# Three PSUM tiles for attention scores and two for the large products, weight sums started behind the first attention, operand forms split by quarters

## The chip, the cores and the metric

The kernel runs on one core of one Trainium2 chip. Its time is the device time of one execution in microseconds (us), the median of three runs. All times below are in us unless marked otherwise.

## The reference

One layer of a hybrid decoder is computed for a prompt of 2048 tokens and for 8 samples of 4 tokens, width 1024, in fp32. Cut to what matters:

```python
h = rms_norm(x, norm_pre_mix)
q, k, v, z1, z2, g_a, g_b = project_inputs(h, w_in, b_gate)   # w_in: 1024 x 5376
for gi, (win, dil) in enumerate(((128, 1), (512, 4), (2048, 16))):
    o, lse = dilated attention of 4 heads of 64 (prompt: banded, sample: against the cache and the new rows)
o_a = merge_dilations(outs, lses)                 # softmax over the three groups' lse
o_b = z1 * (tril(w_spatial) @ layer_norm(z2) + b_spatial)
merged = g_a * (o_a @ w_ao) + g_b * (o_b @ w_bo)  # gates are sigmoids
x = x + rms_norm(merged @ w_out, norm_post_mix)
x = x + rms_norm(square(relu(rms_norm(x, norm_pre_ffn) @ w_up)) @ w_down, norm_post_ffn)
```

The outputs are the new x of prompt and samples, the k and v rows to keep, and the normalised rows of the gMLP.

## The kernel before

The prompt is worked in two halves of 1024 tokens, called stages s = 0 and s = 1; the 32 sample tokens ride with stage 0 (so its chunks are 3 of 352 columns, stage 1's are 2 of 512). Every large product is made of three TensorE matmuls per 128 rows of the contraction: each fp32 operand is split into a high and a low part, and high x high, high x low and low x high are added in PSUM (`gemm`, `gemm_rows`). The order of work is: for each of six head pairs and groups `project` (its v, q and k columns) with the `attention` of the pair before interleaved; `gmlp`; `mix` in stage 0 or `mix_seven` in stage 1 (the gates); `out_rows`; after stage 1 the MLP (`ffn`) for both halves. `mix_seven` and the MLP use a scheme of seven products in place of eight, for which sums of weight quarters (`s1` to `s4`) and differences of activation quarters (`t1`, `v`, `t3`, `t4`) are needed.

**PSUM.** There are eight tiles of 512 fp32 columns: two of tag "t" (transposes), and of the pool `po` three "g" (large products), two "s" (attention scores, and the `w_ao` products of the gates), one "u" (attention values). `bank(kind)` at L204 hands them out in turn: the first matmul of a product waits until the engine that read the tile's last product (ACT or DVE) is done.

**Lanes.** Work that is to lie between the matmuls of the large products is written as Python generators on four lanes. `tick` steps lanes 0 to 2 between rows of a product: lane 0 has the attention, lane 1 the merge, lane 2 the sample attention, whose keys and values come by DMA from the caches (`sample_attention`, DVE lines L919, L920, L956, L967). Lane 3 has `weight_sums`: the sums of weight quarters, made by DMA alone, DRAM to DRAM. A step of it issues one DMA of 512 KB, by turns a copy on SP's queue and an adding DMA on POOL's queue. `pace` (L308) counts the columns of the large products and steps lane 3 each time that another `SUM_EVERY` = 4250 are through. The counter starts at -3 x 4250. What is left over is issued ahead of the MLP.

**The order on the engines** is set by a scheduler that works from the program as written; each engine then takes its instructions in the order in which the scheduler put them.

**Attention.** `scores` (L708, L709) writes the two heads of a unit of 128 queries to one "s" tile; DVE reads it (L710: mask and minimum), ACT makes the exponentials (L714), TensorE transposes them (L742), and `values` (L756) multiplies. `project` writes the keys of the next pair to the two key slots (ACT L575, DVE L576, sample columns L583), which the scores of the pair before must have read. Its own matmuls are those of L322.

**The gates of stage 1.** `mix_seven` first makes the products with `w_ao` and `w_bo` for all eight blocks m, while `forms` makes four difference forms: t3 stays in SBUF, and v, t4 and t1 go by DMA to DRAM (`gt`). Then come 49 products of 12 matmuls (L1235), seven for each of the blocks m = 1 to 7. Each is read by one or two DVE adds (L1242) or an ACT copy (L1240), and gates are made by sigmoids on ACT (L1245). The first 14 products are those of m = 1 and 2 by turns. While they run, `stage` (L1149) brings a form back from DRAM in four quarters of 128 x 512, and `place` splits quarters into high (ACT L349) and low part (DVE L350). `PLACED` says ahead of which product which quarters of which form are split. v is used from product 6 on, t4 from product 8 on, t1 from product 12 on.

Of the kernel before, what the change touches and what calls it, by code (L numbers as in the profile page):

```python
# [42 lines left out]

SUM_EVERY = 4250

# [28 lines left out]

PLACED = {1: (0, (0, 1, 2, 3)), 4: (1, (0, 1)), 5: (1, (2, 3)), 8: (2, (0, 1)), 9: (2, (2, 3))}
FORMS = ("b11", "b21", "b22") + DIFFS
# [36 lines left out]
def hybrid_step(ctx: ExitStack, tc: tile.TileContext, ins: dict, outs: list):  # L113
# [87 lines left out]
    def bank(kind):  # L201
        return po[0].tile([P, 512], F32, tag=kind, bufs={"g": 3, "s": 2, "u": 1}[kind], name="p" + kind)

# [101 lines left out]

    calls = [-3 * SUM_EVERY]

# [707 lines left out]
    def gmlp(s):  # L1015
# [6 lines left out]
        def token_major(m, st):  # L1022
            cs = slice(m * P, (m + 1) * P)
            yield
            for hf in range(2):
# [7 lines left out]
                yield  # L1033
            if s == 0:
                pt = ps.tile([P, 512], F32, tag="t", name="pt")
                nc.tensor.transpose(pt[:NSMP, :P], st[:, HALF:TMAX], ident)
                nc.scalar.activation(zs[:, cs], pt[:NSMP, :P], AF.Gelu)

        def layer_norm():
# [17 lines left out]
            if s == 0:  # L1057
                nc.sync.dma_start(sg_s[0].rearrange("b t c -> (b t) c"), zs)

        def gate(g):  # L1060
# [57 lines left out]
    def mix_seven():  # L1118
# [96 lines left out]
        for n, (m, i) in enumerate(seq):  # L1215
            if n in PLACED:
                place(*PLACED[n])
            if n in (2, 6):
                staged.append(stage(len(staged)))
# [24 lines left out]
            for q, o in done:  # L1244
                nc.scalar.activation(  # L1245
                    X[q], X[q], AF.Sigmoid, bias=b_gate[:, o + m : o + m + 1], scale=-1.0 if o else 1.0
                )
            if i in (4, 6):
                h = halves[i == 6]
                pb = sm.tile([P, 512], F32, tag="e0", name="pbx")  # L1250
                nc.sync.dma_start(pb, pb_d[m][:, h])
                nc.vector.tensor_tensor(out[:, h], out[:, h], a[:, h], ALU.mult)
                nc.vector.tensor_tensor(b[:, h], b[:, h], pb, ALU.mult)
                nc.gpsimd.tensor_tensor(out[:, h], out[:, h], b[:, h], ALU.add)
            if m == 7:

                for ks, h, upto in ((range(8), lo, 1), (range(4), hi, 2), (range(4, 8), hi, 5)):
                    for k in ks:
                        if (k < 7 and i == upto) or (k == 7 and i == (4 if h is lo else 6)):
                            split(act[:, k, 0, h], act[:, k, 1, h], row(order[k])[:, h], nc.vector)  # L1260
# [166 lines left out]
    def weight_sums():  # L1427
# [13 lines left out]
        todo = []  # L1441
        by_rows("w_up", up_d)
        w = ins["w_in"][0]
        ca, cb = (slice(o, o + D) for o in (3328, 4352))
        for q in range(4):
            u, l = slice(q * P, (q + 1) * P), slice(512 + q * P, 512 + (q + 1) * P)
            todo.append(parts(w[u, ca], w[l, ca], w[u, cb], w[l, cb], [gate_d[i, u] for i in range(4)]))
        by_rows("w_down", down_d)
        for n in range(len(todo) + 2):
# [499 lines left out]
```

## Time and profile before

| | |
|---|---|
| median of 3 runs (lowest, highest) | 2857.8 (2856.02, 2861.61) |
| the profiled execution | 2865.88, span 2864.2 |
| TensorE clock granted, mean | 0.995 |
| PE busy | 2810.6 (98%) |
| DVE, ACT, POOL busy | 1366.7 (48%), 1291.4 (45%), 1328.0 (46%) |
| DMA | 550.95 MB, mean 192 GB/s |

The stages lie in the span about so: start to 60, projections and attention of stage 0 to 345, `gmlp` to 430, `mix` to 716, `out_rows` to 836, projections and attention of stage 1 to 1180, `gmlp` to 1276, the first part of `mix_seven` to 1328, its seven-product part to 1470, `out_rows` to 1561, then the MLP. A row of the profile names the line, the engine, the operation and out<-in; an arrow <- behind a time names what ended the wait. PE is TensorE's matmuls, DVE is VectorE, ACT is ScalarE, POOL is GpSimd, and SP issues most DMAs. "x3" is a count.

### The profile page before, as it was taken

The numbers are of one execution on the slowest core, as the hardware profiler recorded it, in microseconds if no ns is written. First come the engines' busy times: TensorE is split into PE (matmuls) and PEld (weight loads), VectorE is DVE, ScalarE is ACT, GpSimd is POOL, SyncE is SP. The second block draws the span as 40 slices with busy tenths as digits, with TensorE's granted clock in tenths as the row PEclk, the third lists the DMA queues.
The fourth block names the chain that finished last, engine by engine and source line by source line (L and its number), as shares of the span: only waits on it lengthen the run. The fifth ranks groups of instructions, "written<-read, shape, count | busy, mean of one in ns | idle before, by whom it ended". The sixth has DMA issues, their size and how long they took to land.

```text
span 2864.2 us, 45829 instructions
## 1 busy us (share of the span) xinstructions
PE 2810.6 (98%) x17350; PEld 2557.5 (89%) x17350; DVE 1366.7 (48%) x2318; ACT 1291.4 (45%) x2519; POOL 1328.0 (46%) x1167
## 2 busy tenths in 40 slices
PE   8999999999999999999999999999999999999998
PEld 8999999999988888877888999999999888888887
DVE  4557555662463444454555546443434644452235
ACT  5344444213553444443446544553434545554333
POOL 3346535464314444344661444445556644445553
PEclk9999999999999999999999999999999999999999
DMA  5566645864667756558456869676656766686655
GB/s 190 162 186 166 174 128 141 227 180 122 203 183 203 209 131 155 126 130 241 136 156 235 283 222 311 191 253 204 203 193 215 223 206 193 190 277 197 191 187 170
DMA packets 486606, 550.95 MB, mean 192 GB/s; under 512 B 28273, under 2 KB 373425, under 8 KB 476658
## 3 DMA queue, kind: packets, MB, share of 16 engines
q1 hardware_dynamic: 472992, 502.60, 54.7%
q0 software_dynamic: 13248, 45.36, 8.8%
q8 instruction: 137, 2.24, 0.3%
q14 instruction: 83, 0.68, 0.1%
q10 hardware_dynamic: 146, 0.07, 0.0%
HBM read 425.54 MB, written 206.27 MB: 221 GB/s over the span
## 4 chain that ended last, share of the span: by engine, by line
PE 50%; DVE 2%; DMA 1%; issue 1%; ACT 1%; POOL 0%; SPq 0%; DVEq 0%; POOLq 0%; ACTq 0%
PE pd L1598 21%; PE pe L1598 11%; PE pe L1706 10%; PE pg L1235 4%; PE pg L336 2%; PE pg L322 1%; PE ps L322 0%; POOL wf L1509 0%; DVE act L350 0%; DMA gt<-gt 0%; PE pt L1310 0%; DMA raw<-in_w_up_dram 0%; ACT junk L395 0%; DMA flat<-hd 0%; DMA f<-ov 0%
## 5 line engine op out<-in xcount | busy, mean ns | idle before, releaser
L1509 POOL TENSOR_TENSOR wf<-raw,wf 128x512 fp32r<-128x512 f32 x493 | 696.6, 1416 | 733.3 <-ACT wf L1508 691.9
L322 PE MATMUL pg<-act,wh 128*128 128x352 f32 (+2 forms) x2976 | 798.6, 347 | 0.8 <-ACT act L349 0.8
L322 PEld LDWEIGHTS pg<-act,wh 128*128 128x128 f32 x2976 | 524.7, 190 | 31.0 <-POOL wl L303 1.1
L1508 ACT CAST wf<-raw 128x512 fp32r<-128x512 f32 x493 | 304.9, 619 | 535.7 <-PE pd L1598 185.7
L322 PE MATMUL pg<-act,wl 128*128 128x352 f32 (+3 forms) x1488 | 513.6, 346 | 0.0
L303 POOL TENSOR_TENSOR wl<-raw,wh 128x512 fp32r<-128x512 f32 (+1 forms) x184 | 242.4, 1345 | 312.9 <-ACT wh L299 270.0
L1598 PE MATMUL pd<-act,wf 128*128 128x264 f32 x2880 | 361.2, 285 | 1.4 <-ACT ov L196 1.0
L1598 PEld LDWEIGHTS pd<-act,wf 128*128 128x128 f32 x2880 | 354.0, 189 | 2.0 <-ACT ov L196 1.4
L322 PEld LDWEIGHTS pg<-act,wl 128*128 128x128 f32 x1488 | 281.5, 189 | 17.1
L1706 PE MATMUL pe<-wf,act 128*128 128x512 f32 (+1 forms) x984 | 224.3, 389 | 1.3 <-ACT wf L1508 1.0
L1706 PEld LDWEIGHTS pe<-wf,act 128*128 128x128 f32 x984 | 181.7, 188 | 43.0 <-ACT wf L1508 1.2
L1607 DVE TENSOR_TENSOR ov<-pd,ov 128x528 f32<-128x528 f32 x140 | 96.2, 704 | 193.5 <-PE pd L1598 188.0
L1598 PE MATMUL pd<-pair,wf 128*128 128x264 f32 x1440 | 183.2, 284 | 0.0
L1598 PE MATMUL pe<-act,wf 128*128 128x512 f32 x768 | 182.6, 392 | 0.1
L1509 DVE TENSOR_TENSOR act<-flat,act 128x1024 fp32r<-128x1024 f32 (+1 forms) x76 | 102.6, 1352 | 164.7 <-ACT act L1508 164.6
L1598 PEld LDWEIGHTS pd<-pair,wf 128*128 128x128 f32 x1440 | 177.9, 188 | 0.0
L1598 PEld LDWEIGHTS pe<-act,wf 128*128 128x128 f32 x768 | 143.8, 188 | 32.9 <-issue 0.3
L299 ACT CAST wh<-raw 128x1024 fp32r<-128x1024 f32 (+1 forms) x91 | 91.9, 1011 | 176.9 <-PE pg L322 101.9
L1607 DVE TENSOR_TENSOR ov<-pe,ov 128x512 f32<-128x512 f32 x136 | 91.5, 687 | 136.9 <-PE pe L1598 126.0
L714 ACT ACTIVATE ov<-ov 128x256 f32<-128x256 f32 (+1 forms) x192 | 91.8, 479 | 115.5 <-DVE ov L710 113.3
L710 DVE CUSTOM_DVE_ANT_0 ov<-ps,con 128x256 f32<-128x256 f32 (+1 forms) x192 | 72.4, 383 | 135.7 <-PE ps L709 124.2
L1598 PE MATMUL pd<-oa,wf 128*128 128x264 f32 x1056 | 135.0, 284 | 0.0
(340 smaller groups left out, 4673.2 us busy)
## 6 DMA issues: line engine op xcount, KB each, us to landing
raw<-in_w_in_dram SPq DMA_DIRECT2D x70, 512.0 KB
raw<-up_sums SPq DMA_DIRECT2D x128, 256.0 KB
raw<-down_sums SPq DMA_DIRECT2D x128, 256.0 KB
flat<-f SPq DMA_DIRECT2D x48, 528.0 KB
raw<-in_w_up_dram SPq DMA_DIRECT2D x96, 256.0 KB
raw<-in_w_down_dram SPq DMA_DIRECT2D x96, 256.0 KB
flat<-f SPq DMA_DIRECT2D x48, 512.0 KB
f<-ov SPq DMA_DIRECT2D x16, 1056.0 KB
```

The source lines that it names most:

```text
L299: nc.scalar.copy(wh[:, :o], raw[:, :o])
L303: eng.tensor_tensor(wl[:, c], raw[:, c], wh[:, c].bitcast(F32), ALU.subtract)
L322: nc.tensor.matmul(pt[:, :n], a[:, o : o + P], b, start=(i == 0 and j == 0), stop=(i == last and j == 2))
L336: nc.tensor.matmul(pt[:n, o : o + width], a, b, start=(i == 0 and j == 0), stop=(i == last and j == 2))
L710: nc.vector.tensor_tensor_reduce(pb[:, h, :w], sp[:, h, :w], mask[:, 2 * P - w : 2 * P], 1.0, 3.0e38, ALU.add, ALU.min, stats[:, u, h : h ...
L714: nc.scalar.activation(pb[:, h, :w], pb[:, h, :w], AF.Exp, scale=-1.0, bias=stats[:, u, h : h + 1], accum_out=stats[:, u, 2 + h : 3 + h],)
L1235: nc.tensor.matmul(pt, w[:, c, k], x[k][:, d], start=k == 0 and j == 0, stop=k == 3 and j == 2)
L1508: nc.scalar.copy(high, raw)
L1509: eng.tensor_tensor(low, raw, high.bitcast(F32), ALU.subtract)
L1598: nc.tensor.matmul(pt[:, o : o + n], w[:, a], x[:, b, c : c + n], start=first and j == 0, stop=last and j == 2)
L1607: nc.vector.tensor_tensor(X[to], res, X[add], ALU.add)
L1706: nc.tensor.matmul(pts[i][:, cs], x[k][:, c, t * P : (t + 1) * P], w[:, d, 0, cs], start=k == 0 and j == 0, stop=k == 15 and j == 2,)
```

## The change

Four things are changed together. (1) The pool `po` has two tiles "g" and three "s" in place of three and two. (2) `pace` starts at -200000 columns and steps every 3600, so that no sum is issued in the projections and the attention of stage 0; and the sums of the gate weights come first, then those of `w_up`, then `w_down`. (3) In `mix_seven` the first form is split one quarter ahead of each of products 1 to 4, the second two quarters ahead of products 6 and 7, the third ahead of 10 and 11; the second and third are fetched at products 4 and 8 instead of 2 and 6, and the first half of a block's rows is finished behind the sixth of its seven products instead of the fifth. (4) `token_major` has one more `yield` ahead of the transpose of the sample columns (stage 0), and `layer_norm` one at its end.

```diff
-SUM_EVERY = 4250
+SUM_EVERY = 3600
-PLACED = {1: (0, (0, 1, 2, 3)), 4: (1, (0, 1)), 5: (1, (2, 3)), 8: (2, (0, 1)), 9: (2, (2, 3))}
+PLACED = {
+    1: (0, (0,)), 2: (0, (1,)), 3: (0, (2,)), 4: (0, (3,)),
+    6: (1, (0, 1)), 7: (1, (2, 3)), 10: (2, (0, 1)), 11: (2, (2, 3)),
+}
     def bank(kind):
-        return po[0].tile([P, 512], F32, tag=kind, bufs={"g": 3, "s": 2, "u": 1}[kind], name="p" + kind)
+        return po[0].tile([P, 512], F32, tag=kind, bufs={"g": 2, "s": 3, "u": 1}[kind], name="p" + kind)
-    calls = [-3 * SUM_EVERY]
+    calls = [-200000]
             if s == 0:
+                yield
                 pt = ps.tile([P, 512], F32, tag="t", name="pt")
                 nc.tensor.transpose(pt[:NSMP, :P], st[:, HALF:TMAX], ident)
             if s == 0:
                 nc.sync.dma_start(sg_s[0].rearrange("b t c -> (b t) c"), zs)
+            yield
-            if n in (2, 6):
+            if n in (4, 8):
                 staged.append(stage(len(staged)))
-            if i in (4, 6):
+            if i in (5, 6):
                 h = halves[i == 6]
                 pb = sm.tile([P, 512], F32, tag="e0", name="pbx")
-                        if (k < 7 and i == upto) or (k == 7 and i == (4 if h is lo else 6)):
+                        if (k < 7 and i == upto) or (k == 7 and i == (5 if h is lo else 6)):
                             split(act[:, k, 0, h], act[:, k, 1, h], row(order[k])[:, h], nc.vector)
         todo = []
-        by_rows("w_up", up_d)
         w = ins["w_in"][0]
         ca, cb = (slice(o, o + D) for o in (3328, 4352))
         for q in range(4):
...
+        by_rows("w_up", up_d)
         by_rows("w_down", down_d)
```

The instructions of each engine are the same in number and kind, but for two loads of an activation table less on ACT; they stand in another order. Lines below `bank` have moved by 3 to 6, so L322 of before is L326 of after, and so on. Three places follow.

PE in stage 1, where one head pair's projection follows another (about 955 to 968 in the span before): ps are score tiles, pg large products, pu values, pt transposes; pair0 and pair1 are the two key slots. pg_9511 and pg_9560 are the two chunks of the next keys, pg_9599 is the first product behind them, and ps_9462 has the last scores that read the old keys. Before:

```order
L322 MATMUL pg_9560<-act_75,wl_9506 128x512
L322 MATMUL pg_9599<-act_75,wh_9593 128x512 x2
L322 MATMUL pg_9599<-act_75,wl_9594 128x512
L322 MATMUL pg_9599<-act_75,wh_9593 128x512 x2
L322 MATMUL pg_9599<-act_75,wl_9594 128x512
L322 MATMUL pg_9599<-act_75,wh_9593 128x512 x2
L322 MATMUL pg_9599<-act_75,wl_9594 128x512
L322 MATMUL pg_9599<-act_75,wh_9593 128x512 x2
L322 MATMUL pg_9599<-act_75,wl_9594 128x512
L756 MATMUL pu_9471<-ov_76 128x64 x2
L708 MATMUL ps_9462<-pair1_8411,oa_77 128x256
L709 MATMUL ps_9462<-pair1_8411,oa_77 128x256
```

Of after, the same place; here pg_9477 and pg_9526 are the two chunks of the next keys and ps_9428 has the last scores of the old ones:

```order
L326 MATMUL pg_9477<-act_75,wl_9472 128x512
L326 MATMUL pg_9526<-act_75,wh_9471 128x512
L760 MATMUL pu_9395<-ov_76 128x64 x4
L746 MATMUL pt_9443<-con_78,ov_76 128x128
L712 MATMUL ps_9407<-pair1_8375,oa_77 128x256
L713 MATMUL ps_9407<-pair1_8375,oa_77 128x256
L712 MATMUL ps_9428<-pair1_8375,oa_77 128x256
L713 MATMUL ps_9428<-pair1_8375,oa_77 128x256
L746 MATMUL pt_9443<-con_78,ov_76 128x128 x3
L326 MATMUL pg_9526<-act_75,wh_9471 128x512
L326 MATMUL pg_9526<-act_75,wl_9472 128x512
L326 MATMUL pg_9526<-act_75,wh_9471 128x512 x2
```

The last scores have moved from the middle of the product behind both chunks to the start of the second chunk, nearly one and a half products ahead.

DVE at the start of the seven-product part of `mix_seven`: L350 (L354) are the splits of form quarters, tiles pair0 to pair3 and oa; L1242 (L1248) are the adds that read a product's PSUM tile pg; L1252 (L1258) multiplies with a gate. The first products there are pg_12683, pg_12710, pg_12739, pg_12757, pg_12783, pg_12804, pg_12832 and so on before, and pg_12659, pg_12681, pg_12704, pg_12724, pg_12756, pg_12773, pg_12798 after. Before:

```order
L350 TENSOR_TENSOR pair1_12671<-gt_12572,pair1_12671 128x512
L350 TENSOR_TENSOR pair1_12671<-gt_12574,pair1_12671 128x512
L1242 TENSOR_TENSOR xt_12674<-pg_12739,xt_12674 128x512
L1252 TENSOR_TENSOR ov_76<-ov_76,xt_12674 128x512
L1242 TENSOR_TENSOR gx_12705<-pg_12757,gx_12705 128x512
L1252 TENSOR_TENSOR ov_76<-ov_76,gx_12705 128x512
L350 TENSOR_TENSOR pair2_12672<-gt_12724,pair2_12672 128x512
L350 TENSOR_TENSOR pair2_12672<-gt_12726,pair2_12672 128x512
L1242 TENSOR_TENSOR xt_12675<-pg_12783,xt_12674 128x512
L350 TENSOR_TENSOR pair3_12673<-gt_12728,pair3_12673 128x512
L350 TENSOR_TENSOR pair3_12673<-gt_12730,pair3_12673 128x512
L1242 TENSOR_TENSOR gx_12706<-pg_12804,gx_12705 128x512
```

Of after:

```order
L1248 TENSOR_TENSOR xt_12651<-pg_12704,xt_12651 128x512
L1258 TENSOR_TENSOR ov_76<-ov_76,xt_12651 128x512
L354 TENSOR_TENSOR pair1_12648<-gt_12548,pair1_12648 128x512
L1248 TENSOR_TENSOR gx_12675<-pg_12724,gx_12675 128x512
L1258 TENSOR_TENSOR ov_76<-ov_76,gx_12675 128x512
L354 TENSOR_TENSOR pair1_12648<-gt_12550,pair1_12648 128x512
L1248 TENSOR_TENSOR xt_12652<-pg_12756,xt_12651 128x512
L1248 TENSOR_TENSOR gx_12676<-pg_12773,gx_12675 128x512
L354 TENSOR_TENSOR pair2_12649<-gt_12741,pair2_12649 128x512
L354 TENSOR_TENSOR pair2_12649<-gt_12743,pair2_12649 128x512
L1248 TENSOR_TENSOR xt_12652<-pg_12798,xt_12652 128x512
L1248 TENSOR_TENSOR xt_12651<-pg_12798,xt_12651 128x512
```

The second form's first splits (pair2) have moved behind the adds of products 4 and 5, and the last two quarters of the first form (pair1) now stand between the adds of products 2, 3 and 4.

ACT at the same place: L349 (L353) is the high part of a quarter, L1508 (L1514) that of a product's weights, L1245 (L1251) the sigmoids with their table load. Before:

```order
L1508 CAST wf_12829<-raw_12826 128x512
L1245 ACT_TABLE_LOAD
L1245 ACTIVATE xt_12674<-xt_12674,b_gate_81 128x512
L349 CAST pair3_12673<-gt_12728 128x512
L349 CAST pair3_12673<-gt_12730 128x512
L1508 CAST wf_12847<-raw_12826 128x512
L1245 ACTIVATE gx_12705<-gx_12705,b_gate_81 128x512
```

Of after:

```order
L353 CAST pair2_12649<-gt_12741 128x512
L1514 CAST wf_12794<-raw_12791 128x512
L1251 ACT_TABLE_LOAD
L1251 ACTIVATE xt_12651<-xt_12651,b_gate_81 128x512
L353 CAST pair1_12648<-gt_12548 128x512
L353 CAST pair2_12649<-gt_12743 128x512
L1514 CAST wf_12817<-raw_12791 128x512
L1251 ACTIVATE gx_12675<-gx_12675,b_gate_81 128x512
```

The first quarter of the second form (gt_12741) now stands ahead of the first sigmoid.

## The prediction

> **What bounds the kernel now.** I read the page first, then the busy time by stage, then the list of waits on PE, and last the timelines around the longest of those waits.
>
> ```profile
> PE 2810.6 (98%) x17350; PEld 2557.5 (89%) x17350; DVE 1366.7 (48%) x2318; ACT 1291.4 (45%) x2519; POOL 1328.0 (46%) x1167
> 0.00:60.00 60.00, 51.85 (x350) 47.20 (x351) 31.46 (x75) 38.69 (x90) 20.11 (x29) 1.00 0.66 209
> 60.00:345.00 285.00, 269.99 (x1828) 261.42 (x1827) 160.58 (x442) 122.62 (x345) 140.17 (x165) 0.99 0.61 167
> 430.00:716.00 286.00, 281.32 (x1749) 278.73 (x1747) 147.21 (x236) 87.49 (x148) 139.86 (x129) 0.99 0.62 167
> 836.00:1180.00 344.00, 342.38 (x2009) 297.86 (x2008) 134.01 (x375) 149.06 (x395) 145.77 (x194) 1.00 0.65 168
> 1328.00:1470.00 142.00, 137.17 (x589) 111.10 (x588) 81.50 (x104) 66.30 (x109) 82.80 (x64) 0.99 0.54 158
> 1561.00:2229.00 668.00, 666.24 (x5488) 665.30 (x5489) 304.37 (x344) 314.21 (x493) 332.67 (x230) 1.00 0.71 232
> ```
>
> The second number of a stage is PE's busy time. PE is the bound: 2864.2 - 2810.6 = 53.6 us of idle are all that an edit of this kind can win, and the change touches no matmul. Stage 0's projections (60 to 345) idle 15.0 us, stage 1's (836 to 1180), the same work without samples, 1.6; the seven-product part (1328 to 1470) 4.8; the MLP's first 668 us, which the change doesn't touch, 1.8. So the question is which waits go and which come. The waits on PE, in sum, times and longest:
>
> ```profile
> PE ps L708 <- DVE ov L710: 13.1, 9, 2.4
> PE pg L1235 <- DVE xt L1242: 4.8, 2, 4.6
> PE ps L322 <- DVE xt L1289: 4.7, 1, 4.7
> PE pt L1069 <- DVE ov L1055: 3.0, 4, 1.0
> PE pt L1036 <- ACT ov L1030: 2.8, 1, 2.8
> PE ps L708 <- DVE lo L814: 0.9, 1, 0.9
> PE pt L618 <- DVE smp L583: 0.7, 1, 0.7
> ```
>
> The first is a score tile that DVE has not read yet, the third the same two tiles in `mix`; no row of this size is a wait of L322 for a product's tile. DVE is late there since it is itself held by the samples' transfers:
>
> ```profile
> 126.75 0.69 DVE L919 TENSOR_TENSOR ov<-xt 128x512 f32<-128x512 f32 x1 [4.29 <-DMA xt<-smp]
> 141.06 0.69 DVE L919 TENSOR_TENSOR ov<-xt 128x512 f32<-128x512 f32 x1 [3.09 <-DMA xt<-in_cache_kv_w_dram]
> 186.66 0.69 DVE L919 TENSOR_TENSOR ov<-xt 128x512 f32<-128x512 f32 x1 [5.50 <-DMA xt<-smp]
> 284.21 0.69 DVE L956 TENSOR_TENSOR ov<-ov,xt 128x512 f32<-128x512 f32 x1 [2.91 <-DMA ov<-in_cache_kv_w_dram]
> 291.26 0.69 DVE L956 TENSOR_TENSOR xt<-xt 128x512 f32<-128x512 f32 x1 [3.54 <-DMA xt<-in_cache_kv_w_dram]
> ```
>
> In brackets stands the idle time before the instruction: five holds of 4.29 + 3.09 + 5.50 + 2.91 + 3.54 = 19.3 us. All that stands behind on DVE waits too, L710 among it. Meanwhile the sums run (first and last start of the issues, and their time to landing):
>
> ```profile
> L1453 SPq DMA_DIRECT2D up_sums<-in_w_up_dram x32: 524/592/3695, 22.1 to 468.9; - x32
> L1458 POOL DMA_DIRECT2D down_sums<-down_sums x16: 751/784/893, 901.9 to 1337.0; - x16
> DMA to landing us min/median/max: 5.1/7.4/12.8
> q0 software_dynamic: 1200, 7.87, 15.0%
> up_sums<-in_w_up_dram SPq DMA_DIRECT2D x17, 512.0 KB
> ```
>
> The last two rows are of 60 to 345 alone, where DMA is 61% busy: 15.0% are the adding DMAs, and 17 copies of 512 KB come on top.
>
> **The change part by part.** The sum is made against the profiled execution, 2865.88; its difference is then applied to the median, which lies 8.1 lower.
>
> *Score waits of stage 0.* The two L708 rows are 13.1 + 0.9 = 14.0. The third tile lets one more pair of scores go ahead, and the sums, 17 copies and about as many adds in this stretch, leave it wholly: the counter now passes zero at 200000 columns, 18 weight blocks of 8 x 1056 = 8448 being 152064, so in `gmlp`. What a transfer costs with and without such company is seen at the gates' forms, each quarter 256 KB:
>
> ```profile
> 1336.69 8.80 DMA gt<-gt
> 1349.78 4.27 SPq L1149 DMA_DIRECT2D gt<-gt  x4
> 1353.18 0.62 ACT L349 CAST oa<-gt 128x512 fp32r<-128x512 f32 x1 [3.24 <-DMA gt<-gt]
> ```
>
> The first, in the chain of waits, took 8.80 from issue to use; the first quarter of the next four was issued at 1349.78 and was used at 1353.18, 3.4 later, when the last sum had been issued (1337.0). A spread of 5.4 is as long as the longest hold. I take 12 of the 14.0. Ends: 4.5 (nine waits, each shortened only by the about 0.5 that a pair's few matmuls give, three taking 0.48 below) and 14.0.
>
> [...]
>
> *Small waits.* L1036 (2.8) is the samples' transpose; its extra `yield` puts more of a product between it and ACT's copies. L618 (0.7) hangs on the same DVE holds. L1069 (3.0) waits for the norm's last steps on DVE; in PE's new order both the transposes ahead of the norm and the gate matmuls behind it stand one product earlier, so it stays. I take 3; ends -1 and 5.
>
> *`mix` of stage 0.*
>
> ```profile
> 612.45 0.69 DVE L956 TENSOR_TENSOR prod<-ov,zs 128x512 f32<-128x512 f32 x1 [4.47 <-DMA ov<-in_cache_kv_w_dram]
> 613.80 0.51 DVE L1289 TENSOR_TENSOR xt<-xt,ps 128x352 f32<-128x352 f32 x1
> 615.43 0.51 DVE L1291 TENSOR_TENSOR xt<-xt,pg 128x352 f32<-128x352 f32 x1
> ```
>
> PE stood 4.7 for the score tile that L1289 read at 613.80. With a third tile it goes on, but the product behind then needs the tile that L1291 gives back at 615.94, 1.6 later, and all PE has for that time is one `w_ao` product of six matmuls, 1.0 by the spacing of the next rows. The wait only changes its name: 0.5 lost; ends +4 and -6 (sums are still under way here, a step each 3600 columns instead of 4250).
>
> *Two product tiles behind the keys.*
>
> ```profile
> 269.05 0.49 PE L322 MATMUL pg<-act,wh 128*128 128x352 f32 x2
> 269.53 0.27 PE L618 MATMUL pt<-con,smp 128*32 128x128 f32 x1
> 277.22 0.49 DVE L576 TENSOR_TENSOR pair<-pg,pair 64x320 fp32r<-64x320 f32 x1
> 277.75 0.19 DVE L583 COPY smp<-pg 128x32 f32<-128x32 f32 x1
> ```
>
> The last chunk of keys ended at about 269.6, and its tile was read by 277.94, 8.3 later. Three matmuls of 352 columns take 0.48, so a product of 24 takes 3.9. Three tiles cover two products, 7.8; two tiles cover one, and 4.4 would show. Of twelve such switches most are better placed in the new order: the last scores of the old keys, which the keys' writing waits for, stand ahead of the second chunk, not inside the product after it. With shorter holds as well I take 3 for all twelve; ends 0 and 10.
>
> *The seven-product part.*
>
> ```profile
> 1328.13 16.66 PE L1235 MATMUL pg<-act,wf 128*128 128x512 f32 x72
> 1344.64 2.96 PE L1235 MATMUL pg<-pair,wf 128*128 128x512 f32 x12
> 1352.17 10.14 PE L1235 MATMUL pg<-pair,wf 128*128 128x512 f32 x36 [4.58 <-DVE xt L1242]
> 1342.96 0.69 DVE L1252 TENSOR_TENSOR ov<-ov,xt 128x512 f32<-128x512 f32 x1 [5.62 <-ACT xt L1245]
> 1343.57 0.68 DVE L1242 TENSOR_TENSOR gx<-pg,gx 128x512 f32<-128x512 f32 x1
> 1347.91 1.24 DVE L1252 TENSOR_TENSOR ov<-ov,gx 128x512 f32<-128x512 f32 x1 [3.65 <-ACT gx L1245]
> ```
>
> Six products took 16.51, so 2.75 each, which is the whole cover that two tiles leave. Product 3 ended at 1339.1, and its add stood at 1343.57 behind L1252, held 5.62 by a sigmoid: product 5, due at 1341.9, would start at 1344.3, 2.4 late. The 4.6 at 1352.17 come from adds behind splits of a quarter in flight. Splits by quarters and adds of products 4 and 5 ahead of them take this wait away, but ACT now has the quarter gt_12741 ahead of the first sigmoid, and products 6 and 7 have their adds behind quarters that can be fetched only when product 3's and 4's splits have freed the tiles: fetched about 10 ahead of use, 8.8 in flight. And the sums are with them now: 160 steps of 3600 from 200000 end at 776000 columns, three or four products before the end of 783872, where before they ended at 160 x 4250 + 12750 = 692750. The part's 49 products of 2048 columns begin at 683520. So some 26 steps lie in it instead of two or three: half on SP's queue among the weights, half on POOL at the 0.78 of the row above (13 x 0.78 = 10 us of a POOL that is busy for 82.8 of 142, so hidden). I take 4.8 growing to 8.3, 3.5 lost; ends +3 (transfers of 3.4) and -10.
>
> *The rest.* At the start and at 1276 to 1328 PE has one product less to run ahead: 1 lost; ends 0 and -5. The order of the sums, gates first, is ready long before `mix_seven` at any rate.
>
> The sum is 12 + 3 - 0.5 - 3 - 3.5 - 1 = 7. From 2865.88 this makes 2858.9, and from the median 2857.8 - 7 = 2850.8, so 2851.
>
> **The rivals.** *Slower: two product tiles become the bound.* Wherever DVE is held, PE now stops one product earlier: 3.9 earlier in stage 0, 2.75 in the gates. The eight holds quoted above (five, 612.45, 1342.96, 1347.91) would cost 6 x 3.9 + 2 x 2.75 = 28.9, against the 15 won: 2857.8 - 15 + 28.9 = 2871.7. It decides from about half of the holds on. For it: the 8.3 of L583, and that the sums now run beside the gates. Against: the order that frees the keys earlier, and that before no product's tile of L322 was waited for at all. [...] Chance 0.23.
>
> *No change: DVE's holds stay and the wait goes to another row.* PE passes the scores and stops at the transposes (L742) or values, which need what DVE and ACT make of the scores. The first term then gives only 4.5: 4.5 + 3 - 0.5 - 3 - 3.5 - 1 = -0.5, or 2858. For it: a tile gives 0.5, a hold lasts up to 5.5. Against: the sums leave the stretch. Chance 0.30.
>
> *More than the sum.* Holds vanish with the sums, nothing new is waited for: 14 + 5 + 0 - 0 - 0 - 0 = 19, or 2839; it lies in the forecast's side.
>
> **How the numbers follow.** A measurement of this kernel can tell about 0.2%, 5.7 us, from no change. The forecast with its better neighbour has 0.47, no change 0.30, slower 0.23. The likeliest case's own range is 2839 to 2852. For 8 in 10 the range reaches from 2838, all ends good, over the rival without change to 2867, where two thirds of the slower rival's way from 2858 is taken.
>
> **What would show it.** Right: the L708 row falls from 13.1 below 3, DVE's holds by `xt<-smp` and cache rows below 3 each, PE's idle time from 60 to 345 falls from 15 to about 5; new rows PE pg L326 <- DVE or ACT stay below 5 in all; L1241's wait is about 8. Wrong: rows of L326 waiting for L580 or L587 (the keys) above 8, or L1241 <- L1248 above 12, make it slower; waits at L746 or L760 of 8 make it no change. It would be wrong in kind if busy time moved: PE's 2810.6 should stay within 5.

## The result and the profile after

The changed kernel takes 2883.4 us (median of 4 runs, 2880.68 to 2891.09) against 2859.7 for the kernel before, run beside it: a ratio of 1.0086, 95% interval 1.0072 to 1.0100. It is slower by about 24. The profiled execution took 2883.0 against 2865.88, so the two profiles show 17.1 of this; that of before lay 6 above its median.

The busy time by engine, from the page of the changed kernel, and its mean clock:

```profile
PE 2816.2 (98%) x17350; PEld 2560.0 (89%) x17350; DVE 1369.0 (48%) x2318; ACT 1286.9 (45%) x2517; POOL 1330.7 (46%) x1167
```

```profile
core 0: 2881.3 us, clock 0.993
```

PE idles 2881.3 - 2816.2 = 65.1 where it idled 53.6, which is 11.5 of the 17.1. The other 5.6 is longer busy time. A part of that is clock: 0.993 in place of 0.995. The records of the granted clock behind this mean know only 1 and 0.50. Up to PE's last matmul they put 23.9 at 0.50 before and 34.1 after, and PE worked for 21.3 and 25.2 of these; taking half of that as lost, an estimate (a product of twelve matmuls took 5.46 below where the clock is 0.50, another of twelve 2.92 at 1.00), it is 10.7 before and 12.6 after. The remaining 3.7 of busy time lies in pieces of at most 1.5 over the stages, and no cause is shown for it.

The busy time by stage of the changed kernel, with stages cut at the same matmuls as before's 60 to 346, 430 to 716, 1328 to 1470 and 1561 to 2178 (length, then PE, PEld, DVE, ACT, POOL, the clock, DMA share, GB/s):

```profile
61.80:338.70 276.90, 268.23 (x1835) 261.64 (x1835) 164.08 (x445) 122.64 (x347) 129.78 (x150) 0.99 0.40 115
420.70:713.50 292.80, 283.24 (x1733) 278.39 (x1733) 146.17 (x227) 85.82 (x144) 142.79 (x130) 0.98 0.63 172
1328.70:1481.30 152.60, 139.78 (x589) 111.90 (x588) 83.95 (x105) 65.59 (x109) 93.50 (x77) 0.97 0.86 224
1573.00:2193.10 620.10, 617.02 (x5064) 616.22 (x5065) 276.86 (x307) 288.44 (x442) 298.09 (x209) 1.00 0.70 231
```

The first stage won: 276.9 in place of 286.0, DMA at 0.40 in place of 0.61. `mix` lost 6.6, the seven-product part 10.4 (its DMA share went from 0.54 to 0.86), and the MLP, which the change doesn't touch, lost 3.8 in its first 616. The list of waits on PE:

```profile
PE pg L326 <- DVE xt L1297: 7.3, 4, 4.0
PE pg L1241 <- DVE gx L1248: 6.9, 1, 6.9
PE ps L712 <- DVE ov L714: 5.0, 5, 2.5
PE pg L1241 <- DVE xt L1248: 4.6, 4, 2.3
PE pd L1604 <- DVE ov L1613: 2.7, 2, 2.1
PE pt L1041 <- ACT ov L1034: 2.4, 1, 2.4
PE pg L326 <- DVE smp L587: 2.0, 2, 1.2
PE pg L340 <- POOL wl L306: 2.0, 1, 2.0
```

The score waits fell from 13.1 to 5.0, and the 4.7 of the score tile in `mix` is gone. In their place stand waits of products for their own tile (pg): 7.3 in `mix`, 2.0 at the keys, 6.9 + 4.6 in the seven-product part. Followed product by product through the trace, PE stood 14 times until a product's tile had been read, 22.8 in sum; before it did so 3 times, 5.2 in sum. The longest one in the timeline:

```profile
1344.30 0.62 ACT L353 CAST pair<-gt 128x512 fp32r<-128x512 f32 x1 [6.54 <-DMA gt<-gt]
1347.50 0.69 DVE L1258 TENSOR_TENSOR ov<-ov,xt 128x512 f32<-128x512 f32 x1 [9.58 <-ACT xt L1251]
1348.71 0.68 DVE L1248 TENSOR_TENSOR gx<-pg,gx 128x512 f32<-128x512 f32 x1
1349.54 5.46 PE L1241 MATMUL pg<-act,wf 128*128 128x512 f32 x12 [6.91 <-DVE gx L1248]
```

ACT waited 6.54 for the first quarter of the second form, whose split stands ahead of the first sigmoid; L1258 on DVE waited 9.58 for that sigmoid; behind it L1248 read the tile of product 3; and product 5 got that tile 6.91 late. That product's twelve matmuls then took 5.46, where the twelve at 1395.14 took 2.92. The clock around this hold:

```profile
1320.00:1345.00 25.00, 22.63 (x99) 18.11 (x97) 3.46 (x5) 8.00 (x15) 9.28 (x8) 1.00 1.00 280
1345.10:1355.30 10.20, 5.76 (x14) 4.54 (x15) 4.08 (x7) 6.47 (x11) 4.52 (x4) 0.50 0.42 125
1355.40:1372.00 16.60, 16.43 (x72) 13.04 (x70) 9.95 (x14) 7.12 (x13) 7.69 (x6) 1.00 0.92 241
```

It is 0.50 for 10.2, from within the hold on, so by the same estimate the hold cost 6.9 and then half of the 5.76 for which PE worked in that stretch, 2.9.

All stages, in the two profiles and in those of six experiments told below (the same matmul cuts them in each):

| stage | before | after | tiles alone | sums alone | after, old tiles | tiles alone, five outside | before, five outside | after, five outside |
|---|---|---|---|---|---|---|---|---|
| start | 60.1 | 61.8 | 62.3 | 60.4 | 59.5 | 63.6 | 59.8 | 62.6 |
| attention, stage 0 | 286.0 | 276.9 | 288.8 | 270.4 | 269.1 | 287.5 | 282.9 | 277.6 |
| `gmlp`, stage 0 | 83.9 | 82.0 | 82.2 | 82.3 | 82.0 | 82.5 | 84.2 | 80.6 |
| `mix` | 286.2 | 292.8 | 293.2 | 286.5 | 291.6 | 284.8 | 285.4 | 285.6 |
| `out_rows`, stage 0 | 119.9 | 119.9 | 121.4 | 119.3 | 119.3 | 117.5 | 117.9 | 119.1 |
| attention and `gmlp`, stage 1 | 439.9 | 438.0 | 440.6 | 437.8 | 437.8 | 440.2 | 440.7 | 436.5 |
| gates, first part | 52.0 | 57.3 | 54.5 | 56.9 | 57.4 | 50.9 | 51.5 | 55.4 |
| gates, seven products | 142.2 | 152.6 | 147.8 | 145.3 | 148.4 | 136.3 | 137.6 | 147.0 |
| `out_rows`, stage 1 | 90.9 | 91.7 | 92.4 | 90.8 | 90.8 | 90.8 | 90.8 | 95.4 |
| MLP | 1302.9 | 1308.3 | 1304.9 | 1303.3 | 1303.4 | 1305.8 | 1302.0 | 1307.6 |

### The profile page after: what moved, and what is told of

Same layout as the page of the kernel before. It is cut to its first block, busy times and chain, and to the rows that moved or that the text cites. A ratio compares the mean times of both kernels' runs of the same rounds, so it can differ in the third digit from the quotient of the medians.

```text
span 2881.3 us, 45761 instructions
## 1 busy us (share of the span) xinstructions
PE 2816.2 (98%) x17350; PEld 2560.0 (89%) x17350; DVE 1369.0 (48%) x2318; ACT 1286.9 (45%) x2517; POOL 1330.7 (46%) x1167
## 5 line engine op out<-in xcount | busy, mean ns | idle before, releaser
L326 PE MATMUL pg<-act,wh 128*128 128x352 f32 (+2 forms) x2976 | 798.4, 348 | 8.2 <-DVE xt L1297 3.4
L326 PEld LDWEIGHTS pg<-act,wh 128*128 128x128 f32 x2976 | 522.2, 190 | 39.6 <-DVE xt L1297 4.4
L1514 ACT CAST wf<-raw 128x512 fp32r<-128x512 f32 x493 | 304.8, 619 | 546.7 <-PE pd L1604 175.4
L326 PE MATMUL pg<-act,wl 128*128 128x352 f32 (+3 forms) x1488 | 512.7, 345 | 0.0
L326 PEld LDWEIGHTS pg<-act,wl 128*128 128x128 f32 x1488 | 281.3, 189 | 17.9 <-issue 0.9
L1604 PEld LDWEIGHTS pe<-act,wf 128*128 128x128 f32 x768 | 144.0, 188 | 32.7 <-issue 0.3
L1604 PEld LDWEIGHTS pd<-oa,wf 128*128 128x128 f32 x1056 | 131.0, 189 | 0.0
```

What stands on the lines that cost most here:

```text
L326: nc.tensor.matmul(pt[:, :n], a[:, o : o + P], b, start=(i == 0 and j == 0), stop=(i == last and j == 2))
L1514: nc.scalar.copy(high, raw)
L1604: nc.tensor.matmul(pt[:, o : o + n], w[:, a], x[:, b, c : c + n], start=first and j == 0, stop=last and j == 2)
```

## The experiments

Four theories stood against each other. *Tiles*: with two product tiles PE has one product of cover (work that it can go on with while a tile is still unread) wherever DVE or ACT is late. *Sums*: their DMAs, moved beside `mix` and the gates, hold DVE and ACT there. *Order*: the new places of the splits do. *Clock*: a hold (a stretch in which an engine stands idle) of over 2 us brings half-clock time with it; in the profile of before each of PE's five holds over 2 (2.10 to 4.68) has a stretch at 0.50 that starts within it or up to 1.4 behind its end. Lines in rows of experiments differ by a few from those above; the names and operations are the same. Ratios are to the kernel before, with 95% intervals.

### One part taken back at a time

The changed kernel with three product and two score tiles:

```diff
-bufs={"g": 2, "s": 3, "u": 1}
+bufs={"g": 3, "s": 2, "u": 1}
```

> The changed kernel, but with three product tiles and two score tiles as before; the sums, the splits and the yields stay changed. Theory 'tiles' (two product tiles leave PE one product of cover wherever DVE or ACT is held): the 6.9 at the first sigmoid of the seven-product part shrinks by one product, 2.75, or more, the waits of the large products in stage 0's mix (7.3) go and a score wait of about 4 to 5 stands there instead; in all 10 to 15 below 2883, so 2868 to 2873. Theory 'sums' (their DMAs now lie beside mix and the seven-product part and hold DVE and ACT): ACT is still held 6 to 7 by the first quarter of the second form, and the time stays above 2876. Theory 'order' (that quarter's split stands ahead of the first sigmoid on ACT): the same hold, the same time. Theory 'clock' (a PE hold of over 2 us is followed by 3.41 us or a multiple at half clock, so it costs 1.7 or more on top): span less PE's idle time less the time lost to the clock is 2807 within 1.5, whatever the rest does.

Measured: 2860.2, ratio 1.0005 (0.9995 to 1.0014). The tiles are worth 23 here, more than the 10 to 15 that their theory asked for, and *sums* and *order* are refuted as the main cause. PE's waits:

```profile
PE pg L1240 <- ACT oa L352: 4.6, 1, 4.6
PE pg L1240 <- DVE xt L1247: 3.2, 3, 1.7
PE ps L711 <- DVE ov L713: 2.9, 5, 1.4
PE ps L325 <- DVE xt L1294: 2.4, 1, 2.4
```

Hardly any product waits for its tile in `mix`; the score waits are lower still, with two tiles. The longest wait left in the seven-product part is one for an operand, the split of the third form. The profile is 22.0 shorter than the changed kernel's: 7.8 in stage 0's attention, 4.9 in the MLP, 4.2 in the seven-product part, 2.3 in the start, and only 1.2 in `mix`, where PE now stands 2.6 for a transpose of the sample attention and 2.4 for a score tile. The clock theory counts PE's idle time up to its last matmul and half of every stretch at 0.50 up to there: 2859.3 - 37.8 idle - 13.7 lost = 2807.8, as it asked.

The changed kernel with the old sums (4250 columns, from -3 x 4250, w_up first):

> The changed kernel with the sums as before (a step every 4250 columns from the start, w_up first). 'Sums': without their DMAs beside the gates, the first quarter of the second form lands early, ACT's hold of 6.5 falls under 4, PE's 6.9 under 3 and the half-clock stretch behind it goes, 7 to 10 less in that part; stage 0's holds of DVE by the samples' transfers come back, 5 to 9 more there; in all 2876 to 2886. 'Tiles' and 'order': the part stays at 13 of idle time, stage 0 gives up its 9, so 2888 to 2893. 'Clock': span less idle less lost clock is 2807 within 1.5.

Measured: 2883.2, ratio 1.0086 (1.0071 to 1.0100), within what *sums* expected: no difference to the changed kernel, because two differences cancel. Stage 0's attention is 287.6 again (276.9 with the new sums), the seven-product part 144.0 (152.6). The new sums win 10.7 in the first and lose 8.6 in the second. Span less idle less lost clock is 2812.7, 6 above the clock theory's figure, a miss.

The changed kernel with the old places of the splits (`PLACED`, n in (2, 6), i in (4, 6), and 4 for the last block):

> The changed kernel with the old places for the splits and fetches of the operand forms. 'Order': the 6.9 and the 5.1 of lost clock behind it go, and the old wait of 4.6 (adds behind the second form's splits), made longer by one product with two tiles to about 7, comes later: 2880 to 2884 if tiles weigh as much, 2874 to 2878 if they don't. 'Sums': DMA is as full at the same time, the wait only moves to another product, within 3 of 2883. 'Clock': span less idle less lost clock is 2807 within 1.5.

Measured: 2885.0, ratio 1.0094 (1.0080 to 1.0108). The seven-product part is 152.6 to the tenth; its longest waits only stand elsewhere. *Order* falls. Span less idle less lost clock is 2805.4, just outside the clock theory's 2807 within 1.5.

The changed kernel without the two yields:

> The changed kernel without the two yields. The wait on the samples' transpose stood at 2.8 before and at 2.4 after, so all theories expect no difference here beyond 2 us around 2883, and the stages behind it as in the changed kernel. It also says whether the MLP, which no part of the change touches, takes 1308.3 as in the changed kernel's profile or 1302.9 as before: if the 5 us there are chance, it lies anywhere between; if they follow from how the stage before it ends, it is 1308.

Measured: 2884.3, ratio 1.0086 (1.0072 to 1.0101), no difference. The MLP took 1307.6.

### One part done alone

The tiles alone, the first diff of these experiments the other way round on the kernel before:

> The kernel before with two product tiles and three score tiles, nothing else changed. 'Tiles': taking the tiles back made the changed kernel 23 faster, and if they cost by themselves, 2859 + 23 = 2882 here. Rival 'together' (two product tiles hurt only where the new places of the sums or splits hold DVE and ACT): 2862 to 2868, with the old wait of 4.6 in the seven-product part one product, 2.75, longer. 'Clock': span less idle less lost clock as before, within 2.

Measured: 2890.4, ratio 1.0100 (1.0083 to 1.0117): the tiles alone cost 28.5 against the 2861.9 of the kernel before in that comparison, more than the whole change. *Together* is refuted. PE's waits:

```profile
PE pg L322 <- DVE xt L1291: 7.0, 4, 4.4
PE pg L1235 <- DVE xt L1242: 6.7, 2, 4.6
PE ps L708 <- DVE ov L710: 5.5, 5, 1.7
PE pg L322 <- DVE smp L583: 4.9, 4, 2.0
PE pg L322 <- ACT xt L1276: 2.2, 2, 1.7
```

Here the third score tile does all that it can, L708 from 13.1 to 5.5, and stage 0's attention is still 2.8 longer: the keys' tile (4.9) and other waits took the place. The profile of this run is 24.0 longer than before's: 4.0 of it up to 430 and in stage 1's attention and `gmlp`, 7.0 in `mix`, 3.0 in both `out_rows`, 8.1 at the gates, 2.0 in the MLP. PE stood 18 times until a product's tile had been read, 25.0 in sum. Span less idle less lost clock is 2810.5 against 2806.4 before, a miss of the clock theory.

Two product and two score tiles, one bank left empty:

> The kernel before with two product tiles and two score tiles; one bank of PSUM stays empty. If the third score tile is worth what the row of the score waits fell by in the changed kernel (13.1 to 5.0), this is 6 to 9 slower than with three score tiles. If that fall came from the sums leaving the stretch, it is within 2 of it. If the loss with two product tiles comes from the third score tile itself (attention running ahead and filling DVE), this is faster than with three, near 2859 to 2865.

Measured: 2884.8, ratio 1.0076 (1.0061 to 1.0091). The row L708 is 10.7 here, so the third score tile halves it; the time does not follow, it is 5.6 lower without that tile (the intervals overlap). None of the three expectations gave this. No worth of the third score tile shows; the lost product tile is the cost.

The new sums alone:

```diff
-SUM_EVERY = 4250
+SUM_EVERY = 3600
-    calls = [-3 * SUM_EVERY]
+    calls = [-200000]
-        by_rows("w_up", up_d)
         w = ins["w_in"][0]
...
+        by_rows("w_up", up_d)
         by_rows("w_down", down_d)
```

> The kernel before with the sums alone as changed (from 200000 columns, a step every 3600, gates first). With three product tiles the changed kernel's profile won 17 from 60 to 430 and gave 15 back in mix, at the start of the gates and in the seven-product part. 'Sums moved, not removed': the same here, so 2856 to 2862, the score waits under 4 and the part from 1276 to 1328 5 longer. Rival 'the old places of the splits suffer more beside the sums': the wait of 4.6 grows to 7 or more, 2862 to 2868. Rival 'the loss in the seven-product part came from the new places': 2848 to 2853.

Measured: 2854.5, ratio 0.9973 (0.9960 to 0.9985): faster than both kernels. Of all that were run, only the two below that build on it are as fast, and the kernel before with five tiles (2856.2, below) lies within its interval. PE's waits:

```profile
PE pg L1235 <- DVE xt L1242: 6.3, 4, 2.8
PE ps L708 <- DVE ov L710: 3.8, 8, 1.0
PE ps L322 <- DVE xt L1289: 3.4, 1, 3.4
```

With two score tiles the row L708 is 3.8, lower than with three in the changed kernel. Stage 0's attention won 15.6; 4.9 and 3.1 went back in the two parts of the gates, as *sums moved, not removed* had it, though the whole lies 1.5 below its range.

The new splits alone:

> The kernel before with the new places of the splits and fetches alone. 'Order helps when DMA is free': the 4.6 goes or halves, 2854 to 2857. 'No worth': another row takes the wait's place (the product on the third form, whose splits now come late, 1355 in the run with three product tiles), 2858 to 2863. The stages ahead of the gates stand as before.

Measured: 2861.3, ratio 0.9996 (0.9986 to 1.0006): no worth, though the 4.6 is gone from the waits and the seven-product part is 1.5 shorter in the profile. With two tiles and the old sums that part takes 147.8 with the old places (the tiles alone) and 144.0 with the new ones (the changed kernel with the old sums); whether the places help there isn't settled by these two profiles.

### Cover or supply

If a hold costs for want of tiles, more tiles must cure it. In the seven-product part no scores are made, so all five of the pool can serve (this is the changed kernel; the pattern for three product tiles is "gsgsg"):

```diff
-            pt = bank("g")
+            pt = bank("gsgss"[n % 5])
```

> The changed kernel, with the products of the seven-product part taking all five tiles in turn (two g, three s; no scores are made there any more), and nothing else changed. 'Cover': what a hold of DVE or ACT costs there is its length less the products that the other tiles hold, 2.75 each; with four in place of one, 11, no hold of this part shows by a tile, and only waits on operands (1.3) and weights stay. The part, 152.6 in the changed kernel, falls to 142 to 145, the whole to 2873 to 2876. Rival 'supply': PE waits there because the splits and weights come late by DMA, and the wait only changes from the tile to an operand: the part stays above 149. The stages ahead stay as in the changed kernel.

Measured: 2881.7, ratio 1.0074 (1.0061 to 1.0087). The part fell only to 149.3, just above the bound of *supply*, and the `out_rows` behind it rose from 91.7 to 96.0, so *supply* holds here. PE's waits and ACT's timeline:

```profile
PE pg L1240 <- ACT oa L352: 7.1, 1, 7.1
PE pg L339 <- DVE xt L1247: 3.1, 2, 1.5
```

```profile
1366.78 1.26 ACT L352 CAST oa<-gt 128x512 fp32r<-128x512 f32 x2 [12.90 <-DMA gt<-gt]
```

No product of the part waits for a tile any more; one waits 7.1 for the split of the third form, for whose fetch ACT stood 12.90. The changed kernel fetches it at product 8, beside the sums.

The same five tiles with the new sums on the kernel before:

> The kernel before with the new sums and five tiles (three g, two s) in turn in the seven-product part. That part had 8.7 of idle time with the new sums and three tiles. 'Cover': four products' cover in place of two leaves under 3 of it: 145.3 falls to 140 to 142, the whole to 2848 to 2851. 'Supply': the waits move to operands, the whole stays at 2854.

Measured: 2853.9, ratio 0.9976 (0.9967 to 0.9985), the same as the new sums alone, as *supply* had it: the part fell from 145.3 to 142.4 and `out_rows` rose from 90.8 to 94.2.

The new sums, a step every 3000 columns:

> The kernel before with the new sums, but a step every 3000 columns, so that the last ends at 680000, ahead of the seven-product part at 683520. 'Sums beside the gates': what the new sums lost there against before, 4.9 from 1276 to 1328 and 3.1 in the seven-product part, comes back in the second place and stays in the first, where the steps still run: 2850 to 2853. Rival: mix and stage 1, with a sixth more sums in the same time, lose as much: 2853 to 2858.

Measured: 2868.1, ratio 1.0021 (1.0011 to 1.0031), 14 slower than every 3600; both expectations missed. `mix` lost 5.6 against the new sums, the first part of the gates 6.4; the seven-product part, free of sums, won only 0.5.

The changed kernel a second time:

> The changed kernel itself, a second time. The MLP took 1308.3 in its first profile and 1302.9 before, with the same order of instructions on every engine. If that is chance of the DMAs, it lies anywhere from 1302.9 to 1308 now; if it follows from two tiles, it is 1308 again. The part from the first product of the seven-product part to its end: 152.6 within 2 if its holds are fixed by the order, 148 to 156 if they hang on when a transfer lands.

Measured: 2886.5, ratio 1.0086 (1.0072 to 1.0101). The seven-product part took 153.7, within 2 of the first profile, and the MLP 1306.9, nearer to the 1308.3 than to the 1302.9.

Then five tiles wherever no scores are made, on two product and three score tiles ("gsgss"; "gsgsg" with three and two). `five` is set behind the drains of `mix` and `mix_seven` and cleared behind `out_rows` of stage 0:

```diff
+    five = [0]
     def bank(kind):
+        if five[0] and kind in "gs":
+            kind = "gsgss"[five[0] % 5]
+            five[0] += 1
```

> Two product tiles and three score tiles on the kernel before, but outside the attention (mix behind its first block, out_rows, mix_seven, where no scores are made) all five tiles in turn serve the products. Two tiles alone cost 28.5; of the 24.0 between the profiles 6.9 lay in mix, 1.5 in out_rows of stage 0, and 2.5, 5.6 and 1.5 at the start of the gates, in the seven-product part and in out_rows behind it. 'Cover': these 18 come back, and more where three tiles waited too, so 2864 to 2872. 'Supply': PE stands there because splits, weights and gates come late, and more tiles only change the name of the wait: 2882 to 2890. The stages of the attention, 60 to 430 and 836 to 1276, stay as with two tiles alone.

Measured: 2861.2, ratio 0.9999 (0.9989 to 1.0009). All of the 28.5 is back. By stage, `mix` and the seven-product part:

```profile
433.70:718.50 284.80, 280.06 (x1733) 276.85 (x1733) 144.51 (x225) 85.03 (x144) 138.68 (x127) 0.99 0.62 168
1327.20:1463.50 136.30, 135.67 (x590) 110.19 (x589) 82.93 (x104) 65.33 (x109) 83.78 (x64) 1.00 0.55 161
```

They stood at 293.2 and 147.8 with two tiles alone; the second now idles 136.30 - 135.67 = 0.6 and has the full clock. Attention stays as long as with two tiles alone, as expected; what it and the start still lose (287.5 and 63.6 against 286.0 and 60.1 before) is made up by the stages with five tiles, which are shorter than before. So *cover* is shown for the stages outside the attention, on the kernel with the old sums.

> The same five tiles outside the attention on the kernel before with the new sums (three product and two score tiles). 'Cover': mix's waits (4.7 of idle time in the run with the new sums) and those of the start of the gates (3.9) shrink, 2846 to 2851. 'Supply': within 3 of the 2854 of the new sums alone.

Measured: 2854.9, ratio 0.9976 (0.9964 to 0.9988): *supply*. Beside the new sums PE waits for weights (5.2 for `wh`; with the new sums alone the longest such wait there was the 1.6 for `wl`).

> The kernel before with the new sums, but a step every 4250 columns instead of 3600: a seventh fewer steps in the same time, and some 23 left over that are issued ahead of the MLP. Steps every 3000 were 14 slower than every 3600, 6 of it at the start of the gates, 3 in the seven-product part and 6 in mix. If it is the density of the sums, this is 2848 to 2853, those places shorter again. Rival: the steps left over stand ahead of the MLP's first weights and make it late: 2856 to 2864, the loss in the MLP's first 190.

Measured: 2874.7, ratio 1.0044 (1.0030 to 1.0059), the rival, and worse than it said. PE's longest wait:

```profile
PE pg L336 <- ACT wh L299: 22.4, 1, 22.4
```

The steps left over stood ahead of the weights of `out_rows`, not of the MLP, and PE waited 22.4 for these. The first part of the gates fell to 51.4, which fits that its loss beside the new sums is a matter of their density.

> The kernel before (three product and two score tiles, old sums) with all five tiles in turn outside the attention. With two product tiles this won 28 and left the stages outside the attention about 9 shorter than before, against about 5 lost in the attention. 'Cover': three tiles there were short too, so 2850 to 2855 here. Rival: what five tiles won came only on top of two; with three the old waits are operands', 2858 to 2862.

Measured: 2856.2, ratio 0.9983 (0.9975 to 0.9991), between the two expectations. Three tiles were a little short too: the seven-product part fell from 142.2 to 137.6, `out_rows` of stage 0 by 2.0.

> The changed kernel with all five tiles in turn outside the attention. 'Cover': what two product tiles cost there comes back, 2858 to 2864 from 2883 to 2886, a bit less than on the kernel before (28), since the new sums hold DVE, ACT and the weights there. 'Supply': with the new sums the operands are late, as in the run of five tiles in the seven-product part alone: 2872 or more.

Measured: 2867.0, ratio 1.0023 (1.0014 to 1.0033), between the two expectations: 16 to 20 of the changed kernel's loss are cover. What stays lies in the seven-product part and behind it:

```profile
PE pg L1246 <- ACT oa L357: 3.9, 1, 3.9
PE ps L344 <- DVE xt L1253: 2.6, 2, 2.4
```

The first is again the late third form.

> The kernel before with five tiles outside the attention and sums from 100000 columns (two thirds through the attention of stage 0), a step every 3600, gates first: the last step is at 676000, ahead of the seven-product part, and no denser than in the new sums. If the sums lose at the start of the gates and in the seven-product part by lying beside them, this wins 6 to 8 there over the new sums and gives up 3 to 5 in the last third of the attention: 2848 to 2853. If DMA beside mix and stage 1 decides, 2854 to 2860.

Measured: 2863.6, ratio 1.0010 (1.0000 to 1.0020), slower than either expectation. The two parts of the gates did about as the first said: 8.7 shorter than with the new sums alone, all of it in the seven-product part (135.4, no idle time), though five tiles have a share in that. But stage 0's attention took 284.5, 14 more than with sums that start behind it, in a profile that lies 8.3 above its median. Most of this stands in its last third: PE idles 7.75 of 94.5 there, all for two score tiles, while DVE waits 5.3 and 1.8 for the samples' cache rows; the DMA share is 0.65 and the clock 0.93. With the new sums alone PE idles 1.05 of 85.8 there, at 0.43 and 1.00. That the sums delay these cache rows is the likely reading; one profile doesn't show it.

## Why the prediction was wrong

The forecast was a gain of 7; it became a loss of 24. The sign was lost in one step: **two product tiles**.

- *Two product tiles behind the keys* ("I take 3 for all twelve; ends 0 and 10"), with the 0.5 of `mix`, the 1 of the rest and a share of the 3.5 of the gates, put some 6 on the tiles. Alone they cost 28.5, in the changed kernel 23. At the keys themselves the term was about right: PE waited 2.0 there, 4.9 with the tiles alone. What failed is that a tile less was priced at the key switches and hardly elsewhere. The argument that failed is the one set against the slower rival, "that before no product's tile of L322 was waited for at all" (there was one wait, of 0.4). A wait that is absent says that three tiles left no shortage, not how much was left over. That could have been taken from the trace of before: of its 318 tiles of products, 40 have their first matmul ahead of the end of the last reading two products earlier, by 115 us in sum. One is in the prediction's own rows: product 6 began at 1344.64, and the tile of product 4 was read only just ahead of 1352.17, since the product that started then had waited for it. That is an upper figure: when one product is held, the next ones come later too, and the scheduler makes another order for two tiles. With the tiles alone 18 waits of 25.0 in sum came of it.
- *The rival* of two product tiles as the bound was the right mechanism. That its price agrees, 28.9 against the 28.5 measured, is partly luck: it put 5 x 3.9 = 19.5 on stage 0's attention, 3.9 on `mix` and 5.5 on the gates; with the tiles alone these stages grew by 2.8, 7.0 and 8.1 (in the attention the score waits fell at the same time), and 3.0 came in `out_rows` and 2.0 in the MLP. It was weighed too low, and set against 15 won where the sums alone win 7.4 and, with two tiles, nothing.
- *Score waits of stage 0* (12): the stage won 9.1, the row fell to 5.0, not below 3, and PE's idle time there to 8.7, not 5. But the cause is the sums, not the tile: with two score tiles and the new sums the stage wins 15.6, with three and the old sums it loses 2.8. DVE's holds by the samples' transfers fell, though not below 3 each (the longest is 5.1).
- *`mix`* (0.5): the wait changed its name as foreseen, L322 <- L1289 to L326 <- L1297. The size failed: 6.6, in four waits of products for their tile and 1.5 more half-clock loss. Five tiles there bring it to 284.8 and 285.6, less than before; three product tiles, with the rest of the change, leave it at 291.6, so the tiles are not all of it.
- *The seven-product part* (3.5): 10.4. The mechanism was right, ACT held by the quarter ahead of the first sigmoid, and so was the place; but this is a matter of cover and of sums at once. The old tiles take 4.2 off it, the old sums 8.6, the old splits nothing.
- *The rest* (1): 5.3 at the first part of the gates, and 4.9 with three product tiles, so the sums, which the term left out there.
- *Small waits* (3): L1041 stayed at 2.4, so its yield bought nothing, while the 3.0 of L1069, which "stays", went. It also went without the yields and with the tiles alone. Without the yields the time is the same.
- *Busy time* "should stay within 5": it rose by 5.6. Matmuls at half clock are 1.9 of it by the estimate above, a term that the sum didn't have; the rest is unexplained.
- *The signs of being wrong* did not show, though the kernel became slower: L326 waited 2.0 for the keys (the sign was 8), and L1241 <- L1248 came to 6.9 + 4.6 = 11.5 (the sign was 12). The sign of being right that failed was "below 5 in all" for new waits of L326: `mix` alone has 7.3.
- *The MLP*, 5.4, was not foreseen, and no cause is shown. Its instructions stand in the same order on every engine. Over 20 profiles it took 1302.0 to 1308.3: 1302.8 to 1308.3 with two product tiles, 1302.0 to 1305.8 with three. Whether anything but when transfers land decides that stays open.

## What to carry to other kernels

Before a buffer is taken from a pool, work out from the trace for each use how long ahead of need its predecessor comes free, now with one buffer less; this gives an upper figure (115 here, where 28.5 came), while a list of waits shows only where the present number is already short. Work that DMA does in the background is moved, not removed (here the sums alone won 15.6 in stage 0's attention and lost 8.0 at the gates): price the stage that receives it like the stage that it leaves. And when a part of a change is said to help, run it alone: here one part won 7 and another lost 28.

## What the runs showed of the hardware

A short hold can cost more than its length, by estimate 3.8 in place of 2.1 here. The first four lines cut the changed kernel's MLP around a hold of 2.14, the last is `out_rows` of stage 0, which has one of 2.0:

```profile
1785.80:1788.90 3.10, 3.10 (x26) 2.90 (x24) 2.56 (x3) 2.48 (x5) 2.39 (x3) 1.00 0.29 108
1789.00:1791.10 2.10, 0.00 (x0) 0.02 (x1) 2.10 (x3) 0.10 (x1) 0.80 (x1) 1.00 0.77 243
1792.30:1795.60 3.30, 3.30 (x18) 3.30 (x17) 1.48 (x3) 2.72 (x6) 1.75 (x2) 0.50 1.03 316
1795.70:1800.00 4.30, 4.30 (x37) 4.30 (x37) 4.18 (x4) 0.62 (x1) 2.70 (x2) 1.00 1.07 378
713.50:833.40 119.90, 117.90 (x803) 105.95 (x802) 68.96 (x108) 68.11 (x187) 22.92 (x19) 1.00 0.58 199
```

PE did nothing for 2.1, worked at full clock for another 1.2, then 3.4 at 0.50, and at full clock again; put down to the hold, that makes 3.8 of 2.1 (half of 3.4 on top, as in the estimate above). In `out_rows` a hold of 2.0 had no such stretch, and the clock is 1.00 throughout. In the two traces of before and after, up to PE's last matmul, the stretches at 0.50 last 3.41 five times and 6.83 once before, 3.41 twice, 6.83 once and 10.24 twice after, and their starts lie whole multiples of 3.413 apart (in that of before 15, 58, 64, 35 and 182). Which hold has one does not follow from its length: in the changed kernel those of 2.14, 2.47, 3.96 and 6.91 have one, those of 2.00, 2.01, 2.26 and 2.37 have none, and one of 1.74 has one of 6.83. Before, a stretch of 3.41 starts at 731.3 with no hold over 0.17 in the 12 ahead of it. So the 2 us of the clock theory was the author's estimate, and what brings such a stretch is not shown. Over the 20 profiles, span less PE's idle time (up to its last matmul) less half of the time for which PE worked at 0.50 is 2805 to 2814, while the spans run from 2852 to 2888: idle time and the clock account for most of the differences, by the same estimate. Of the 24.0 between the profiles of the tiles alone and of before they are 11.3 and 7.9 (18.5 lost in place of 10.7), so the clock is about a third.
